# One GpSimd power instruction per small reciprocal square root, in a kernel of two float32 transformer blocks

## The chip, the cores and the metric

The kernel runs on one core of one Trainium2 chip. The metric is the device time of one execution in microseconds (us): the median of three runs before the change is 1636.81 us (1635.35 to 1637.84). A core has a matrix engine (TensorE; PE in the rows, with its weight loads as PEld), three engines for elementwise work (VectorE, DVE; ScalarE, ACT; GpSimd, POOL) and a queue for transfers (SyncE, SP). Each engine takes its instructions in a fixed order and waits on semaphores for what others make.

## What is computed

Two blocks of two layers each, on 256 tokens of 1024 features, with batch 1, all in float32. The first block puts 16 meta tokens ahead, so it works on 272. Each of its layers is a mixer (a gated delta rule and a sparse attention side by side, gated) and a gated feed-forward network with a convolution; the second block has one layer of dilated attention beside a gated convolution, one of retention, and a feed-forward network behind each. What matters here is that every layer normalises by roots of means or sums of squares:

```python
def rms_norm(x, g):
    xf = x.astype(jnp.float32)
    y = xf * lax.rsqrt(jnp.mean(xf * xf, axis=-1, keepdims=True) + EPS)
    return (y * g.astype(jnp.float32)).astype(x.dtype)

def l2_norm(x):
    xf = x.astype(jnp.float32)
    return xf * lax.rsqrt(jnp.sum(xf * xf, axis=-1, keepdims=True) + EPS)
```

```python
for l in range(DEPTH):
    n = rms_norm(h, norm_mix[l])
    h = h + hybrid_mixer(n, ...).astype(h.dtype)
    n = rms_norm(h, norm_ffn[l])
    h = h + conv_gated_mlp(n, w_up[l], conv_ffn[l], w_down[l]).astype(h.dtype)
```

## The kernel before

The residual stream lies in SBUF in eight tiles of 128 features by 272 (later 258 or 256) tokens. Every large product is a loop over tiles of 128 features of the weight: `raw` loads a piece of 1 MB from HBM into one of two buffers, `parts` splits it into a high part `whi` (ScalarE, L256) and a low part `wlo` (VectorE, L257), four buffers of each, and `mm3` makes three matmuls of each pair of tiles (L276, L277, L278), so that the sum is nearly exact in float32. These matmuls, 256 to 272 columns wide, are most of the program.

The norm is pulled apart (`Norm`). The products start at once on the stream times the gain (`xh`, `xl`), and the factor of each token comes beside them: ScalarE squares, VectorE adds (L162), TensorE sums over the features by a product with ones (L168), VectorE turns the sum into the mean `nrm_u` (L170), `rsqrt` makes the factor `nrm_y`, and TensorE casts it to all partitions (`rowcast`, L352), from where ScalarE copies it as `rB`. What leaves a product is multiplied by `rB`.

`rsqrt` is called 32 times, each for a tile of 128 partitions (16 for the meta tokens) by 1 to 16 elements: for the 8 norms (`nrm`), in each of the two `mixer1` for the index keys (`ri`), the delta rule's keys (`rk`), the attention's keys (`rka`) and queries (`qsc`) and three times for the outputs of the delta rule (`ors`), in `even_mixer` for keys and queries (`erk`, `erq`), and twice for each of the four heads of `retention_mixer` (`brv`). Each call takes the bit pattern of its operand as a first guess (L247) and makes three Newton steps of three instructions each (L249, L250, L251), all on VectorE, each needing the one before.

The small work runs in chains that `tick` steps between the products. The order of each engine's queue isn't the source's: the tile framework's scheduler sets it when the program is built, from priorities and its own estimates of when each instruction can start, so another way of making a factor moves work around it on every engine.

Of the kernel before, what the change touches and what calls it, by code (L numbers as in the profile page):

```python
# [11 lines left out]
F32 = mybir.dt.float32  # L12
# [108 lines left out]
def bc(ap, n):  # L121
    """[p, a] -> [p, a, n], the last axis with stride 0."""
    return ap.unsqueeze(2).to_broadcast([ap.shape[0], ap.shape[1], n])


def mid(ap, n):
    """[p, a] -> [p, n, a], the middle axis with stride 0."""
    return ap.unsqueeze(1).to_broadcast([ap.shape[0], n, ap.shape[1]])


class Norm:
    """RMS norm of the residual stream: parts X of h*g at once; the mean u of the squares with eps, the factor r of
    each row, and rB, the factors on every partition, come from a chain that runs beside the first products."""
# [56 lines left out]
class K:  # L190
    def __init__(self, ctx, tc, ins, out):
# [6 lines left out]
        self.chains, self.later, self.held = [], [], None  # L198

# [20 lines left out]
    def evict(self):  # L220
        """Emits what takes the last product out of PSUM: a tile late, for the priority of the products."""
# [19 lines left out]
    def rsqrt(self, u, n, tag, bufs=None, rows=P):  # L241
        """1/sqrt of the small tile u[:, :n], from the bit pattern and three Newton steps."""
        V = self.nc.vector
        yi = self.small(n, tag + "_y", I32, bufs)
        a, b = self.small(n, "nwt_a")[:rows], self.small(n, "nwt_b")[:rows]
        y, u = yi.bitcast(F32), u[:rows]
        V.tensor_scalar(yi[:rows], u.bitcast(I32), -0.5, 1597463007.0, OP.mult, OP.add)  # L247
        for _ in range(3):
            V.scalar_tensor_tensor(a, y[:rows], -0.5, y[:rows], OP.mult, OP.mult)  # L249
            V.tensor_tensor(b, a, u, OP.mult)  # L250
            V.scalar_tensor_tensor(y[:rows], b, 1.5, y[:rows], OP.add, OP.mult)  # L251
        return y

    def split(self, hi, lo, src):
        """hi + lo == src, both float32r; src in SBUF or PSUM."""
# [3 lines left out]
    def raw(self, src, nk, nc_):  # L259
        """src [128, nk * nc_] of a laid out weight -> SBUF."""  # L260
# [4 lines left out]
    def parts(self, v):  # L265
        """A [128, k, c] piece of a weight -> its float32r parts."""
# [13 lines left out]
    def dense(self, w, X, ev, ncols=256, raw=None, kstep=8):  # L280
        """A unit [128, k * ncols] of a weight times X of up to 8 k tiles, outputs feature-major, one at a time."""
# [19 lines left out]
    def pieces(self, w, nkt):  # L301
        """The parts of a unit of 256 columns, four k tiles at a time."""
# [6 lines left out]
    def dense_pair(self, w, X, ev, tag, ahead=()):  # L309
        """A unit of 256 columns times X of many k tiles, two outputs at a time; ahead: pieces that are there already."""  # L310
# [12 lines left out]
    def dense_ts(self, w, X, ev, tag):  # L323
        """X (two token tiles) times a unit of 512 columns, outputs token-major."""
# [24 lines left out]
    def rowcast(self, ps, col, seg):  # L349
        """ps[:, token] = the column's value of the token, on every partition."""  # L350
# [5 lines left out]
    def ffn(self, hv, N, lead, w_up, conv, w_down, both, done=None):  # L356
        """lead: columns of X ahead of the tokens that are kept (they feed the gate's convolution alone)."""
# [58 lines left out]
def in_turn(*gens):  # L416
    """A chain whose steps are a step of each of the generators."""
# [10 lines left out]
def by_turns(*gens):  # L428
    """A chain that steps one of the generators at a time."""
# [10 lines left out]
def mixer1(k_, l, h, N, final, first=None):  # L440
# [33 lines left out]
    def stats(src, rows, at, key):  # L474
        """Sums of squares over the features, token-major, in columns of stat."""
# [13 lines left out]
    # small projections: index key (64), index weights (8), decay (4), beta (4)  # L489
# [3 lines left out]
    def small_chain():  # L493
# [9 lines left out]
        # index keys, on both halves of the partitions  # L503
# [20 lines left out]
        # decay and beta  # L524
# [1064 lines left out]
```

## Time and profile before

| | us |
|---|---|
| runs, median of 3 | 1636.81 |
| the profiled execution, span from first to last instruction | 1633.0 |
| TensorE busy in it | 1616.9 (99%) |
| VectorE busy | 1228.8 (75%) |
| ScalarE busy | 881.7 (54%) |
| GpSimd busy | 17.9 (1%) |
| mean granted clock of TensorE | 0.993 of full |

The span is the profiled execution's own; the run's time holds what lies around it as well. Busy time of an engine says only that it had an instruction in work. Which engine sets the end is read from the chain of waits and from what TensorE waits for. A clock column of 1.00 stands for 2.4 GHz, of 0.50 for 1.2 GHz; a matmul then takes twice as long.

### The profile page before, as it was taken

The page shows a single profiled execution, that of the slowest core. Times are in us where ns is not written, and L with a number is a line of the kernel's source. Part 1 is how long each engine was busy: PE and PEld are TensorE (multiplying, and loading weights), DVE is VectorE, ACT ScalarE, POOL GpSimd, SP SyncE. Part 2 cuts the span into 40 slices and gives each one's busy share as a digit, 9 for nine tenths or more (in the row PEclk, how much of TensorE's full clock was granted, in tenths as well). Part 3 has the DMA queues.
Part 4 walks back from the last instruction along what each step waited for, and adds up shares of the span by engine and source line. Part 5 has one row for each costly group of instructions (what it writes and reads, how often), then busy time and mean ns, then how long its engine had stood idle before and what let it go on. Part 6 is the DMA issues. An engine that isn't in the chain of part 4 may idle for free.

```text
span 1633.0 us, 31727 instructions
## 1 busy us (share of the span) xinstructions
PE 1616.9 (99%) x12702; PEld 1551.1 (95%) x12702; DVE 1228.8 (75%) x2653; ACT 881.7 (54%) x1534; POOL 17.9 (1%) x174
## 2 busy tenths in 40 slices
PE   7999999999999999999999999999999999999999
PEld 7989899999999989999999998999999888999999
DVE  6788578888557887588886549899956767689963
ACT  5565455555445664555554456566644444556642
POOL 0000000000000000000000000000000000000000
PEclk9999999999999999999999999999999999999999
DMA  5432235445553322245555543455555454545553
GB/s 207 155 113 74 100 107 178 164 173 180 163 185 130 130 104 78 78 155 181 181 181 187 200 173 128 165 185 194 175 182 186 161 175 155 174 173 194 184 183 127
DMA packets 38452, 258.00 MB, mean 158 GB/s; under 512 B 4384, under 2 KB 6816, under 8 KB 9120
## 3 DMA queue, kind: packets, MB, share of 16 engines
q1 hardware_dynamic: 37440, 253.79, 44.7%
q8 instruction: 100, 1.64, 0.4%
q10 hardware_dynamic: 864, 2.18, 0.3%
q14 instruction: 48, 0.39, 0.1%
HBM read 254.90 MB, written 1.05 MB: 157 GB/s over the span
## 4 chain that ended last, share of the span: by engine, by line
PE 96%; DVE 3%; ACT 1%; issue 0%; DMA 0%; SPq 0%; ACTq 0%; DVEq 0%
PE psd L276 20%; PE psd L277 20%; PE psd L278 20%; PE pss L276 3%; PE pss L278 3%; PE pss L277 3%; PE psn L276 3%; PE psn L278 3%; PE psn L277 3%; PE psn L752 1%; PE stat L481 1%; PE psd L338 1%; PE psd L339 1%; PE psd L340 1%; PE psn L339 1%; PE psn L338 1%
## 5 line engine op out<-in xcount | busy, mean ns | idle before, releaser
L256 ACT ACTIVATE whi<-raw 128x1024 fp32r<-128x1024 f32 (+1 forms) x487 | 508.3, 1044 | 569.6 <-PE psd L277 329.5
L257 DVE TENSOR_TENSOR wlo<-raw,whi 128x1024 fp32r<-128x1024 f32 (+1 forms) x487 | 585.6, 1203 | 223.2 <-ACT whi L256 218.3
L276 PE MATMUL psd<-xh,whi 128*128 128x256 f32 (+2 forms) x2384 | 695.6, 292 | 6.0 <-ACT whi L256 6.0
L278 PE MATMUL psd<-xh,wlo 128*128 128x256 f32 (+2 forms) x2384 | 684.2, 287 | 0.7 <-DVE wlo L257 0.7
L277 PE MATMUL psd<-xl,whi 128*128 128x256 f32 (+2 forms) x2384 | 682.8, 287 | 0.0
L276 PEld LDWEIGHTS psd<-xh,whi 128*128 128x128 f32 x2384 | 453.6, 190 | 13.9 <-ACT whi L256 6.0
L277 PEld LDWEIGHTS psd<-xl,whi 128*128 128x128 f32 x2384 | 455.1, 191 | 3.3 <-issue 1.7
L278 PEld LDWEIGHTS psd<-xh,wlo 128*128 128x128 f32 x2384 | 453.3, 190 | 1.8 <-DVE wlo L257 1.2
L278 PE MATMUL pss<-ah,wlo 128*128 128x256 f32 (+1 forms) x352 | 99.9, 284 | 0.0
L278 PE MATMUL psn<-ah,wlo 128*128 128x256 f32 (+1 forms) x352 | 99.9, 284 | 0.0
L276 PE MATMUL pss<-ah,whi 128*128 128x256 f32 (+1 forms) x352 | 99.9, 284 | 0.0
L276 PE MATMUL psn<-ah,whi 128*128 128x256 f32 (+1 forms) x352 | 99.9, 284 | 0.0
L277 PE MATMUL psn<-al,whi 128*128 128x256 f32 (+1 forms) x352 | 99.7, 283 | 0.0
L277 PE MATMUL pss<-al,whi 128*128 128x256 f32 (+1 forms) x352 | 99.7, 283 | 0.0
L276 PEld LDWEIGHTS pss<-ah,whi 128*128 128x128 f32 x352 | 66.5, 189 | 0.0
L276 PEld LDWEIGHTS psn<-ah,whi 128*128 128x128 f32 x352 | 66.5, 189 | 0.0
L277 PEld LDWEIGHTS pss<-al,whi 128*128 128x128 f32 x352 | 66.5, 189 | 0.0
L277 PEld LDWEIGHTS psn<-al,whi 128*128 128x128 f32 x352 | 66.5, 189 | 0.0
L278 PEld LDWEIGHTS pss<-ah,wlo 128*128 128x128 f32 x352 | 66.2, 188 | 0.0
L278 PEld LDWEIGHTS psn<-ah,wlo 128*128 128x128 f32 x352 | 66.2, 188 | 0.0
L374 ACT ACTIVATE gy<-gu,prm 128x256 f32<-128x256 f32 (+1 forms) x88 | 43.5, 498 | 3.9 <-DVE gu L371 3.7
L376 DVE SCALAR_TENSOR_TENSOR gy<-gu,prm,gy 128x256 f32<-128x256 f32 (+1 forms) x88 | 42.8, 487 | 2.1
(401 smaller groups left out, 2450.2 us busy)
## 6 DMA issues: line engine op xcount, KB each, us to landing
raw<-in_w_up_dram SPq DMA_DIRECT2D x44, 1024.0 KB, 4.8
raw<-in_ffn_w_up_dram SPq DMA_DIRECT2D x44, 1024.0 KB, 4.8
raw<-in_w_in_dram SPq DMA_DIRECT2D x26, 1024.0 KB, 4.8
raw<-in_w_gate_dram SPq DMA_DIRECT2D x16, 1024.0 KB, 4.8
raw<-in_w_down_dram SPq DMA_DIRECT2D x16, 1024.0 KB, 4.9
raw<-in_ffn_w_down_dram SPq DMA_DIRECT2D x16, 1024.0 KB, 4.9
raw<-in_even_w_in_dram SPq DMA_DIRECT2D x10, 1024.0 KB, 4.8
raw<-in_w_out_dram SPq DMA_DIRECT2D x8, 1024.0 KB, 4.7
```

Of the source, the lines that this page charges most:

```text
L256: self.nc.scalar.activation(hi, src, AF.Copy)
L257: self.nc.vector.tensor_tensor(lo, src, hi.bitcast(F32), OP.subtract)
L276: mm(ps, w[0], x[0], start=first, stop=False)
L277: mm(ps, w[0], x[1], start=False, stop=False)
L278: mm(ps, w[1], x[0], start=False, stop=last)
L338: mm(ps[m], h, hi[:, k, :], start=(kk == 0), stop=False)
L339: mm(ps[m], h, lo[:, k, :], start=False, stop=False)
L340: mm(ps[m], l, hi[:, k, :], start=False, stop=(kk == nkt - 1))
L374: A.activation(y, u[:, o:o + T], AF.Copy, scale=conv(0, c))
L376: V.scalar_tensor_tensor(y, u[:, o + 2:o + 2 + T], conv(2, c), y, OP.mult, OP.add)
L481: mm(stat[:n, at(s):at(s) + 1], sq[:rows, o:o + n], c["ones"][:rows, 0:1], start=True, stop=True)
L752: mm(cols(p3, w, a, 4)[:, hh], R[:n, hh, :n], cols(Z, w, a, 4)[:, hh], start=True, stop=True)
```

## The change

`rsqrt` no longer runs on VectorE. One GpSimd instruction (`tensor_tensor` with the operation `pow`) raises the tile to -0.5; the exponent is a column `mhalf` of -0.5, set once on GpSimd and read with stride 0. The rest of the diff takes comments and docstrings out, which shifts line numbers: a line of the kernel after from 252 on is 4 less than before (L256 is L252, L352 is L348).

```diff
@@ class K, __init__ @@
         self.chains, self.later, self.held = [], [], None
+        self.mhalf = self.cp.tile([P, 1], F32, name="mhalf")
+        self.nc.gpsimd.memset(self.mhalf, -0.5)
...
     def rsqrt(self, u, n, tag, bufs=None, rows=P):
         V = self.nc.vector
-        yi = self.small(n, tag + "_y", I32, bufs)
-        a, b = self.small(n, "nwt_a")[:rows], self.small(n, "nwt_b")[:rows]
-        y, u = yi.bitcast(F32), u[:rows]
-        V.tensor_scalar(yi[:rows], u.bitcast(I32), -0.5, 1597463007.0, OP.mult, OP.add)
-        for _ in range(3):
-            V.scalar_tensor_tensor(a, y[:rows], -0.5, y[:rows], OP.mult, OP.mult)
-            V.tensor_tensor(b, a, u, OP.mult)
-            V.scalar_tensor_tensor(y[:rows], b, 1.5, y[:rows], OP.add, OP.mult)
+        y = self.small(n, tag + "_y", F32, bufs)
+        self.nc.gpsimd.tensor_tensor(y[:rows], u[:rows], self.mhalf[:rows, 0:1].to_broadcast([rows, n]), OP.pow)
         return y
```

Every engine has the same instructions as before but for these: VectorE loses 320, GpSimd gains 32 `pow`, the memset of `mhalf` and one instruction that loads code (ISA), ahead of the first `pow`. Their order differs. Three places follow, in the built programs' order.

TensorE at the norm that begins layer 1 of the first block, before the change. `sacc` holds the summed squares, `psd` is a product's accumulator, `nrm_y` the factor. First the sums of the norm:

```order
L168 MATMUL pss_6049<-g0_77,sacc_6014 16x1
L168 MATMUL pss_6049<-g0_77,sacc_6014 128x1 x2
L278 MATMUL psd_6076<-xh3_5962,wlo_6073 128x272
L276 MATMUL psd_6076<-xh4_5966,whi_6072 128x272
L277 MATMUL psd_6076<-xl4_5967,whi_6072 128x272
```

The row cast comes 33 wide matmuls after the sums, and the last of them before it are these:

```order
L278 MATMUL psd_6111<-xh5_5970,wlo_6108 128x272
L276 MATMUL psd_6111<-xh6_5974,whi_6107 128x272
L277 MATMUL psd_6111<-xl6_5975,whi_6107 128x272
L352 MATMUL pss_6090<-g0_77,nrm_y_6056 128x16
L352 MATMUL pss_6090<-g0_77,nrm_y_6056 128x128 x2
```

The same place on TensorE after the change (L272 to L274 are the wide matmuls, L348 is the row cast):

```order
L168 MATMUL pss_5952<-g0_79,sacc_5917 16x1
L168 MATMUL pss_5952<-g0_79,sacc_5917 128x1 x2
L274 MATMUL psd_5968<-xh3_5865,wlo_5965 128x272
L272 MATMUL psd_5968<-xh4_5869,whi_5964 128x272
L273 MATMUL psd_5968<-xl4_5870,whi_5964 128x272
L274 MATMUL psd_5968<-xh4_5869,wlo_5965 128x272
L348 MATMUL pss_5982<-g0_79,nrm_y_5959 128x16
L348 MATMUL pss_5982<-g0_79,nrm_y_5959 128x128 x2
L272 MATMUL psd_5968<-xh5_5873,whi_5964 128x272
```

Four wide matmuls are left between the sums and the row cast. Counted at the eight norms in their order, 23, 25, 33, 25, 24, 26, 60 and 26 matmuls stood between before, and 0, 12, 4, 11, 4, 11, 5 and 4 stand there now.

VectorE in the retention mixer, at the first head's first group norm. `buv` is the variance with its epsilon, `brv_y` the factor, `bnb` the negative mean times the factor. Before:

```order
L1365 TENSOR_TENSOR buv_16167<-bmv_16165,repu_16108 128x1
L247 TENSOR_SCALAR brv_y_16169<-buv_16167 128x1
L249 SCALAR_TENSOR_TENSOR nwt_a_16170<-brv_y_16169 128x1
L250 TENSOR_TENSOR nwt_b_16171<-nwt_a_16170,buv_16167 128x1
L251 SCALAR_TENSOR_TENSOR brv_y_16169<-nwt_b_16171,brv_y_16169 128x1
...
L1368 SCALAR_TENSOR_TENSOR bnb_16182<-bmv_16165,brv_y_16169 128x1
L257 TENSOR_TENSOR wlo_16340<-raw_16337,whi_16339 128x1024
```

And after:

```order
L1361 TENSOR_TENSOR buv_15916<-bmv_15914,repu_15857 128x1
L1364 SCALAR_TENSOR_TENSOR bnb_15920<-bmv_15914,brv_y_15918 128x1
L253 TENSOR_TENSOR wlo_16067<-raw_16064,whi_16066 128x1024
L1357 BN_STATS bst_15945<-pss_15942 128x6
L1359 BN_AGGR bmv_15947<-bst_15945 128x2
```

The ten instructions are gone from between `buv` and `bnb`, and `bnb` needs the factor that GpSimd makes; the split of a weight stands behind it.

GpSimd at the program's start, after the change (before, the first memset of `xp` stood first here, and there was no row of L247):

```order
L200 MEMSET mhalf_67 128x1
L572 MEMSET xp_300 128x3
L632 MEMSET sel0_1402 128x16
L632 MEMSET sel1_1652 128x16
L247 ISA
L247 TENSOR_TENSOR nrm_y_208<-nrm_u_206,mhalf_67 128x3
L247 TENSOR_TENSOR ri_y_286<-ui_284,mhalf_67 128x3
L572 MEMSET xp_373 128x3
```

The code load stands ahead of the first `pow`, and memsets for the convolutions stand behind the second.

## Rows read from the trace of the kernel before

**Rows 1.** The page: busy us, share of the span, count by engine; chain that ended last.

```profile
PE 1616.9 (99%) x12702; PEld 1551.1 (95%) x12702; DVE 1228.8 (75%) x2653; ACT 881.7 (54%) x1534; POOL 17.9 (1%) x174
...
PE 96%; DVE 3%; ACT 1%; issue 0%; DMA 0%; SPq 0%; ACTq 0%; DVEq 0%
```

**Rows 2.** Waits of PE and PEld: who waited for what, total us, times, longest us.

```profile
PE psd L276 <- ACT whi L256: 6.0, 1, 6.0
PE psd L278 <- DVE wlo L257: 0.7, 1, 0.7
...
PEld pss L352 <- DVE nrm_y L251: 1.4, 5, 0.3
PEld psx L1385 <- DVE on L1376: 0.7, 1, 0.7
```

**Rows 3.** Windows: length, busy us by engine, granted clock, DMA share, GB/s.

```profile
14.00:21.20 7.20, 6.49 (x30) 6.14 (x30) 4.91 (x28) 1.41 (x4) 0.00 (x0) 0.53 0.71 269
41.50:45.10 3.60, 3.60 (x19) 3.60 (x18) 3.60 (x6) 1.94 (x3) 0.00 (x0) 0.53 0.30 73
516.00:523.00 7.00, 6.61 (x44) 5.95 (x43) 5.71 (x14) 3.02 (x6) 0.10 (x1) 0.51 0.48 153
604.80:608.30 3.50, 3.50 (x18) 3.50 (x18) 2.12 (x9) 1.78 (x9) 0.00 (x0) 0.51 0.75 274
```

**Rows 4.** Timeline of PE ahead of two of these: start us, us, instruction, count.

```profile
40.18 0.39 PE L560 MATMUL psn<-g_g,g 128*128 128x8 f32 x2
...
514.54 0.38 PE L559 MATMUL psn<-g_g,g 16*128 16x4 f32 x2
```

**Rows 5.** Whole span, one line of the kernel each (L247, then L251): DVE busy.

```profile
0.00:1633.00 1633.00, 5.16 (x32) 0.99 0.46 158
...
0.00:1633.00 1633.00, 15.09 (x96) 0.99 0.46 158
```

**Rows 6.** Waits of DVE, the longest.

```profile
DVE wlo L257 <- ACT whi L256: 218.3, 209, 3.5
```

**Rows 7.** Timeline of DVE at the first group norm of retention.

```profile
1272.99 0.15 DVE L247 TENSOR_SCALAR brv_y<-buv 128x1 int32<-128x1 int32 x1
...
1274.93 0.16 DVE L1368 SCALAR_TENSOR_TENSOR bnb<-bmv,brv_y 128x1 f32<-128x1 f32 x1
```

**Rows 8.** Timeline of DVE and PE at the norm of layer 1.

```profile
483.47 0.37 PE L278 MATMUL psd<-xh,wlo 128*128 128x272 f32 x1
483.65 0.16 DVE L170 TENSOR_SCALAR nrm_u<-pss 128x3 f32<-128x3 f32 x1 [0.88 <-PE pss L168]
483.99 1.22 DVE L257 TENSOR_TENSOR wlo<-raw,whi 128x1024 fp32r<-128x1024 f32 x1
484.06 0.29 PE L276 MATMUL psd<-xh,whi 128*128 128x272 f32 x1
487.74 0.16 DVE L251 SCALAR_TENSOR_TENSOR nrm_y<-nwt_b,nrm_y 128x3 f32<-128x3 f32 x1
487.95 0.28 PE L352 MATMUL pss<-g,nrm_y 16*128 16x16 f32 x1
```

**Rows 9.** Groups by form: busy us, mean ns of one, idle before.

```profile
L370 POOL MEMSET gu<- 128x2 f32 x88 | 8.5, 99 | 898.4 <-DVE gy L376 323.9 <-DVE h L1417 271.3 <-DVE sacc L162 183.5
L775 POOL MEMSET Y<- 128x512 f32 x4 | 2.1, 525 | 131.1 <-PE psn L752 131.1
L143 ACT ACT_TABLE_LOAD x1 | 1.3, 1283 | 3.5 <-DMA h<-in_xT_dram 3.5
```

**Rows 10.** Timeline at the start.

```profile
0.77 0.16 POOL L636 MEMSET sel<- 128x16 f32 x2
14.97 0.57 PE L276 MATMUL psd<-xh,whi 128*128 128x272 f32 x1
15.15 0.16 DVE L170 TENSOR_SCALAR nrm_u<-pss 128x3 f32<-128x3 f32 x1 [1.05 <-PE pss L168]
16.76 0.29 PEld L278 LDWEIGHTS psd<-xh,wlo 128*128 128x128 f32 x1 [1.01 <-DVE wlo L257]
```

## Prediction

> **What bounds the kernel now.** I read the page first: TensorE is busy 1616.9 of 1633.0 us, VectorE 75%, GpSimd 1%, and the chain that ended last runs 96% through TensorE [rows 1]. So a change on VectorE or GpSimd moves the time only where TensorE waits for it, or where it alters the clock that TensorE is granted. Next the waits of TensorE, product side and weight-load side [rows 2]: the largest is the 6.0 us at the start, which nothing here touches. Those that end with VectorE are 0.7 us for `wlo`, 0.7 us for `on`, and 1.4 us, in 5 pieces, of row casts (L352) waiting for the last Newton step (L251). That 1.4 us is all that the chains which the change replaces cost directly; with `on` and the sub-microsecond waits beside it, there are about 2 us to win from waits. Last the windows of the granted clock [rows 3]: four stretches stand at about half (1.2 of 2.4 GHz), 7.2, 3.6, 7.0 and 3.5 us long. The work in them takes twice its time, so they hold some 10 us. Shortly before the second and the third, TensorE ran the small matmuls with 4 and 8 columns (L559, L560) [rows 4].
>
> **What goes.** There are 32 calls of `rsqrt`: 8 norms, 7 in each of the two `mixer1` (14), 2 in `even_mixer`, 8 in `retention_mixer`. Each loses one L247 and three each of L249, L250 and L251, which take the same time: 5.2 + 3 x 15.1 = 50.4 us of VectorE [rows 5]. On the end's path lies only the 1.4 us above. VectorE has cover to spare: it waits 218.3 us for `whi` [rows 6], which says that it is ahead of its supply.
>
> As a delay the chain matters more than as busy time. In retention, where nothing stands between the steps, L247 starts at 1272.99 and the user of the result, L1368, at 1274.93: 1.94 us [rows 7]. At the norm of layer 1 other work is woven in: the mean `u` is written at 483.81 and the last Newton step at 487.90, and the row cast starts at 487.95 [rows 8]. One hand-over between engines thus takes 0.05 us.
>
> **What comes.** One `pow` on GpSimd for each of the 32, over 1 to 16 elements a partition, one memset, and a code load ahead of the first. No row shows a `pow`; call its length p. From below: a GpSimd memset of 2 elements takes 99 ns, one of 512 takes 525 ns, so the element count is no term here and an instruction cannot be shorter than about 0.10 us [rows 9]. [...] I take 1.0 us, the middle, since it has more in common with the chain than with a memset. I know no reason that rules out either end.
>
> **Where p stands on the path.** The order of TensorE's queue moves with the change, and this is the term that decides. Before, 23 to 60 matmuls stood between the sums of a norm (L168) and its row cast (L352). Now, in the order of the eight norms, it is 0, 12, 4, 11, 4, 11, 5, 4. At the norm of layer 1 the rows price it: the first matmul behind the sums starts at 483.47 and the fifth at 484.06, so TensorE would come to the row cast about there, while `u` is written at 483.81 [rows 8]. With two hand-overs the factor is there at 483.91 + p, so TensorE waits p - 0.15. Each further matmul takes off 0.12 to 0.13.
>
> - Three norms with 4 matmuls: 3 x (1.0 - 0.15) = 2.55 us.
> - One with 5: 0.73 us.
> - Two with 11 and one with 12: seven or eight more matmuls, about 0.9 to 1.0 us; the wait is p - 1.05 or less, nothing at p = 1.0.
> - The first, with none: TensorE is through the sums at 14.97, `u` is written at 15.31 [rows 10], so it waits p + 0.44 = 1.44 us. But 1.01 us was lost there already, waiting for `wlo` [rows 10], and VectorE can make that meanwhile; I count 0.43.
>
> Sum 3.71 us, less the 1.4 us that the row casts waited before: +2.3 us. Other row casts (`ri`, `rka`) and the transposes of `erk` keep at least some ten matmuls of cover, and cost nothing at p = 1.0.
>
> **VectorE's own waits.** At 19 places (`srk` 2, `nqs` 2, `od` 6, `eqs` 1, `bnb` 8) the user of the factor is on VectorE and now stands next to, or one or two instructions behind, what makes `u`. VectorE then stands for p + 0.1 with everything behind it in its queue, `wlo` among it, which TensorE wants. It stood 1.94 us in the chain before, so this is a gain up to p of about 1.8 and I cost it at nothing; the 218.3 us of waiting for `whi` are the cover [rows 6]. Without that cover each 0.1 us over 1.8 would cost 1.9 us over the 19 places.
>
> **GpSimd's queue.** It is in order, and a memset behind a `pow` now waits with it. These memsets (174 instructions, 17.9 us) run far ahead of their users and GpSimd is idle 99% [rows 1], so nothing. The code load stands after two `sel` memsets that start at 0.77 us and end at 0.93, and does not wait for VectorE; `u` comes at 15.31 [rows 10]. It has 14.4 us of cover. The nearest row of a load of functions is ScalarE's table, 1.28 us [rows 9]. Nothing for it, then.
>
> The Trainium skill, GPSIMD Engine Reference, section 2.1 (Instruction dispatch), gives about 6 us for the code load of a first call; by that estimate the load ends near 7 us, and the sum stays. No run here shows it yet.
>
> **The forecast.** 1633.0 + 2.3 = 1635.3 us of span. The median of the runs is 1636.81, 3.8 us over the span of the profiled execution, for what lies around it; so 1639.1 us. Between the ends: p = 0.10 removes the 1.4 us and adds no wait, 1635.4; p = 1.94 gives 1.37 + 3 x 1.79 + 1.67 + 2.5 (the three long ones) - 1.4 = +9.5, 1646.3. From p = 1.2 on the change is slower by over 0.2% (3.3 us, about what a measurement of this kernel can tell from none).
>
> **Rivals.**
>
> - *A dear power.* Software on GpSimd takes 1.3 us or more, and TensorE stands at the eight row casts: 1641 at 1.3, 1646 at 1.94; at 3 us, 8 places x 1.06 more and 19 places of 1.1 us on VectorE, of which a part shows, 1655. For it: nothing in the trace bounds a software loop. Against: the operands are tiny.
> - *Fewer half-clock stretches: faster.* In the new order the six matmuls of L559 and L560 stand in layer 0 behind 24 wide products, where two stood between them and the sums (L481) ahead; in layer 1 the small matmuls L704 and L713 of the first segment move away from them. If the second and third stretch vanish, half of 3.6 + 7.0 us comes back: 1639.1 - 5.3 = 1633.8, and with a power of 0.7 us (1637.6 by the sum) 1632.3. It decides if those windows show the full clock. Against: stretches of this kind also arise elsewhere.
> - *More half-clock stretches.* Sums, a wait of about 1 us and the row cast now stand together at four norms. TensorE fell to half around sums and a wait at the start [rows 3, 10]. Two new stretches of 3.5 us cost 3.5 us, of 7 us 7 us: 1642.6 to 1646.
> - *The power waits for VectorE.* `wlo` stands in VectorE's queue directly behind `u` (or one small instruction later) and takes 1.22 us [rows 8]. If GpSimd could not read its operands while it runs, a power issued late would wait up to 1.22 us more: 4 x 1.22 at the short norms, 4.9 us, so 1644.0. Against: `wlo` started at 483.99, 0.18 us after `u` was written, so the power would be first. A code load that takes over 14.4 us goes with this case; it costs its excess once.
>
> On that the Trainium skill, SBUF — State Buffer, section "SBUF: two separate sides", says that GpSimd and a VectorE instruction with two operands in SBUF take one shared pair of ports in turn, each for its whole length. `wlo` reads two SBUF tiles, so the rule speaks against this change: by it whichever starts first holds up the other. The trace of before has no GpSimd instruction that reads, so it cannot bear it out.
>
> **How the numbers follow.** Forecast (p from 0.7 to 1.3, the clock as it was) 0.42: 1637.6 to 1641.3, two thirds of it within 0.2%. Dear power 0.22. Faster by the clock 0.13, of which 0.02 stays within 0.2%. More half clock 0.12. Power or code load held up 0.11, of which 0.04 stays within. That gives faster 0.11, same 0.28 + 0.02 + 0.04 = 0.34, slower 0.55. The predicted time is that of the likeliest case, 1639. The forecast alone spans 1637 to 1642; the range that should hold 8 in 10 reaches down to the faster clock, 1632, and up into the dear power, 1652.
>
> **What would show it.** In the profile after: the length of L247 on GpSimd (step p); the waits of TensorE's weight load at the row cast on GpSimd's `nrm_y`, which should come to about 4 us at 4 to 5 norms; VectorE's waits on `brv_y`, `ors_y`, `srk`, about 1.1 us each with `wlo` still in time; VectorE busy near 1178 us; and the windows of half clock, four of them as before. It is wrong if the power is over 1.3 or under 0.5 us, if the waits at the row casts are not there, or if the sum of half-clock time differs by over 3 us.

## The result, and the profile after

The changed kernel takes 1649.1 us against 1636.7 before: ratio 1.0077, 95% interval 1.0063 to 1.0092. The kernel after once more (e9 below) gave 1648.8 against 1637.0, ratio 1.0076 (1.0063 to 1.0088). It is slower by 12 us; the forecast was 1639.0. The sign and the range (1632 to 1652) held, the size did not: +12.4 us for +2.3.

In the kernel after, the line numbers behind the removed lines are 4 lower: the products are L272 to L274, the split `whi` is L252, the subtraction `wlo` L253, the row cast L348. L247 is now the power.

The page, as in [rows 1]: busy us, share of the span of 1649.7 us, count, by engine.

```profile
PE 1623.1 (98%) x12702; PEld 1555.0 (94%) x12702; DVE 1196.3 (73%) x2333; ACT 882.5 (53%) x1534; POOL 54.8 (3%) x207
```

The span grew by 16.7 us (1633.0 to 1649.7, the slowest of the four executions; the others lie between 1645.4 and 1647.4, and the medians differ by 12.4 only). Of it TensorE is busy 6.2 longer with the same 12702 matmuls, and stands 10.5 longer (1633.0 - 1616.9 = 16.1 before, 26.6 after). VectorE lost 32.5 us of work and nothing came of it.

Where TensorE stands, as in [rows 2]: who waits for what, total us, times, longest.

```profile
PE pss L348 <- POOL nrm_y L247: 4.5, 4, 2.3
PE psn L729 <- DVE XT L717: 2.4, 2, 1.2
...
PE psn L888 <- DVE od L883: 1.9, 2, 1.0
PE pss L1202 <- POOL up L1243: 1.7, 1, 1.7
PE psn L852 <- DVE W L838: 1.0, 2, 0.5
PE pss L1161 <- DVE att L1163: 0.8, 1, 0.8
PE pss L348 <- POOL xp L572: 0.6, 1, 0.6
```

In the kernel before none of these places stood over 0.2 us on the product side. The names "up" and "xp" are memsets that happen to follow a power in GpSimd's queue; what TensorE waited for there is the power (`erk_y`, `nrm_y`), as the timelines below show. So 5.1 us are row casts of norms, and 7.8 us are waits inside the mixers that the prediction had put at nothing.

How long a power takes: groups of L247 by form, busy us, mean ns of one, idle before. `qsc` and `rk` have 12 elements a partition, `erk` and `erq` 16, `ors` 4, `brv` 1.

```profile
L247 POOL TENSOR_TENSOR rk_y<-uqk,mhalf 128x12 f32<-128x12 f32 x2 | 4.5, 2266 | 33.9 <-DVE uqk L897 33.9
...
L247 POOL TENSOR_TENSOR brv_y<-buv,mhalf 128x1 f32<-128x1 f32 x8 | 4.4, 544 | 144.2 <-DVE buv L1361 144.2
L247 POOL TENSOR_TENSOR ors_y<-ouo,mhalf 128x4 f32<-128x4 f32 x4 | 4.0, 1008 | 103.6 <-DVE ouo L881 103.6
...
L247 POOL TENSOR_TENSOR erk_y<-euk,mhalf 128x16 f32<-128x16 f32 x1 | 2.9, 2896 | 9.9 <-DVE euk L1195 9.9
L247 POOL TENSOR_TENSOR ors_y<-ouo,mhalf 16x4 f32<-16x4 f32 x2 | 2.0, 999 | 6.4 <-DVE ouo L881 6.4
```

From 544 ns at one element to 2896 at sixteen is (2896 - 544) / 15 = 157 ns for each further element; four elements give 544 + 3 x 157 = 1015 by that, against 1008, and twelve give 2271, against 2266 for `rk` (`qsc` takes 2390; as it starts, VectorE is in work on two tiles, see e1). Sixteen partitions take as long as 128 (999 and 1008).

One of the new waits in full, at `rk` of the first mixer: timeline of GpSimd, VectorE and TensorE (start us, length, instruction, idle before and releaser).

```profile
81.48 2.27 POOL L247 TENSOR_TENSOR rk_y<-uqk,mhalf 128x12 f32<-128x12 f32 x1 [17.04 <-DVE uqk L897]
83.78 0.17 DVE L901 TENSOR_TENSOR srk<-rk_y,uqk 128x12 f32<-128x12 f32 x1 [2.12 <-POOL rk_y L247]
84.02 1.22 DVE L253 TENSOR_TENSOR wlo<-raw,whi 128x1024 fp32r<-128x1024 f32 x1
85.16 0.64 DVE L712 SCALAR_TENSOR_TENSOR MT<-psn,bet,QT 16x16 f32<-16x16 f32 x4
86.52 0.21 DVE L717 TENSOR_TENSOR XT<-XT,g 16x64 f32<-16x64 f32 x1
86.78 0.25 PE L729 MATMUL psn<-g,XT 16*16 16x16 f32 x4 [1.21 <-DVE XT L717]
```

`srk` stands 2.12 us for the power, and VectorE's queue stands with it: a subtraction, `MT` and `XT` come late, though none of them uses `srk`. TensorE then waits 1.21 us for `XT`. The same happens in layer 1.

The half-clock stretches (windows: length, busy us by engine, granted clock, DMA share, GB/s), as in [rows 3], the first and three that stand behind a new wait:

```profile
13.70:23.80 10.10, 7.79 (x36) 7.64 (x37) 4.54 (x18) 2.59 (x7) 2.77 (x3) 0.50 0.36 126
88.80:92.20 3.40, 3.40 (x27) 3.12 (x24) 2.11 (x4) 1.99 (x5) 0.00 (x0) 0.51 0.38 96
...
559.80:563.20 3.40, 3.40 (x21) 3.12 (x22) 2.07 (x7) 1.73 (x5) 0.00 (x0) 0.50 0.23 46
...
1460.90:1464.30 3.40, 3.40 (x17) 3.40 (x18) 0.43 (x1) 0.89 (x2) 0.00 (x0) 0.50 0.00 0
```

There are seven in this execution (the others start at 143.4, 525.7 and 614.4), with 28.2 us of TensorE's work in 30.6 us; before, four with 19.4 in 20.5. What half clock costs is somewhat less than half: wide matmuls of 272 columns start every 0.125 us at the full clock (483.68 to 484.06 in [rows 8]) and every 0.227 us at half (89.76 to 91.58 here), 1.8 times and not twice as long. So a stretch of 3.4 us loses about 1.5 us, and the 8.8 us of work more in such stretches come to some 4 of the 6.2 us that TensorE was busy longer (estimates from these spacings).

### The profile page after: what moved, and what is told of

Read it like the earlier page. It is cut to its first block, busy times and chain, and to the rows that moved or that the text cites. A ratio compares the mean times of both kernels' runs of the same rounds, so it can differ in the third digit from the quotient of the medians.

```text
span 1649.7 us, 31460 instructions
## 1 busy us (share of the span) xinstructions
PE 1623.1 (98%) x12702; PEld 1555.0 (94%) x12702; DVE 1196.3 (73%) x2333; ACT 882.5 (53%) x1534; POOL 54.8 (3%) x207
## 4 chain that ended last, share of the span: by engine, by line
PE 88%; issue 5%; DVE 4%; POOL 1%; ACT 1%; DMA 1%; SPq 0%; POOLq 0%; DVEq 0%; ACTq 0%
PE psd L272 18%; PE psd L273 18%; PE psd L274 18%; PE pss L272 3%; PE pss L273 3%; PE pss L274 3%; PE psn L273 3%; PE psn L272 3%; PE psn L274 3%; PE psn L748 1%; DVE wlo L253 1%; PE psn L335 1%; PE psn L334 1%; PE psn L336 1%; PE stat L477 1%
## 5 line engine op out<-in xcount | busy, mean ns | idle before, releaser
L252 ACT ACTIVATE whi<-raw 128x1024 fp32r<-128x1024 f32 (+1 forms) x487 | 507.9, 1044 | 558.2 <-PE psd L273 329.7
L253 DVE TENSOR_TENSOR wlo<-raw,whi 128x1024 fp32r<-128x1024 f32 (+1 forms) x487 | 585.3, 1203 | 236.7 <-ACT whi L252 231.3
L272 PE MATMUL psd<-xh,whi 128*128 128x256 f32 (+2 forms) x2384 | 696.0, 292 | 6.2 <-ACT whi L252 6.2
L274 PE MATMUL psd<-xh,wlo 128*128 128x256 f32 (+2 forms) x2384 | 684.0, 287 | 0.3 <-DVE wlo L253 0.3
L272 PEld LDWEIGHTS psd<-xh,whi 128*128 128x128 f32 x2384 | 453.7, 191 | 14.9 <-ACT whi L252 6.2
L274 PEld LDWEIGHTS psd<-xh,wlo 128*128 128x128 f32 x2384 | 453.2, 190 | 1.8 <-issue 0.9
L272 PE MATMUL pss<-ah,whi 128*128 128x256 f32 (+1 forms) x352 | 99.8, 283 | 0.0
L274 PE MATMUL pss<-ah,wlo 128*128 128x256 f32 (+1 forms) x352 | 99.8, 283 | 0.0
L274 PE MATMUL psn<-ah,wlo 128*128 128x256 f32 (+1 forms) x352 | 99.7, 283 | 0.0
L272 PE MATMUL psn<-ah,whi 128*128 128x256 f32 (+1 forms) x352 | 99.7, 283 | 0.0
L272 PEld LDWEIGHTS pss<-ah,whi 128*128 128x128 f32 x352 | 66.5, 189 | 0.0
L272 PEld LDWEIGHTS psn<-ah,whi 128*128 128x128 f32 x352 | 66.4, 189 | 0.0
L274 PEld LDWEIGHTS psn<-ah,wlo 128*128 128x128 f32 x352 | 66.2, 188 | 0.0
L274 PEld LDWEIGHTS pss<-ah,wlo 128*128 128x128 f32 x352 | 66.2, 188 | 0.0
L367 DVE TENSOR_TENSOR gu<-psd,rB 128x256 f32<-128x256 f32 (+2 forms) x88 | 37.4, 425 | 15.0 <-PE psd L274 9.6
```

Of the source, the lines that this page charges most:

```text
L252: self.nc.scalar.activation(hi, src, AF.Copy)
L253: self.nc.vector.tensor_tensor(lo, src, hi.bitcast(F32), OP.subtract)
L272: mm(ps, w[0], x[0], start=first, stop=False)
L274: mm(ps, w[1], x[0], start=False, stop=last)
L367: V.tensor_tensor(u[:, 2:2 + n], ps, N.rB, OP.mult)
```

## The experiments

Four questions: does the length of the power cost the time, or the new order of the queues? Which powers? Do GpSimd and VectorE hold each other up? Does a first call cost something? In e1 to e9 the order of the instructions on TensorE, VectorE and ScalarE is exactly that of the kernel named (after, or before in e2), so that only the stated thing differs.

**e1: the order of the kernel after, with a short instruction.**

```
-            V.memset(ps[:, 0:1], 1e30)
+            V.memset(ps[:, 0:1], 1.0)
...
-        self.nc.gpsimd.memset(self.mhalf, -0.5)
+        self.nc.gpsimd.memset(self.mhalf, 0.05)
...
-        self.nc.gpsimd.tensor_tensor(y[:rows], u[:rows], self.mhalf[:rows, 0:1].to_broadcast([rows, n]), OP.pow)
+        self.nc.gpsimd.tensor_tensor(y[:rows], u[:rows], self.mhalf[:rows, 0:1].to_broadcast([rows, n]), OP.mult)
```

> The kernel after with a product by a constant, 0.05, where each power stood (and 1.0 for the 1e30 of padded rows, so that all numbers stay finite; the factors are therefore not the roots). TensorE, VectorE and ScalarE run their instructions in exactly the order of the kernel after; only the length of the 32 GpSimd instructions changes. Theory A (the length of the power, at places where somebody stands for it): TensorE's waits for GpSimd (about 5 us at row casts, 1.7 at the transposes of erk) and the waits of VectorE for rk, qsc, ors, erq shrink to a few tenths each, the half-clock stretches that follow such a wait (88.8, 559.8, 1460.9) go, and the time falls from 1649.1 to 1637 to 1641. Theory B (the new order of the queues itself, with the clock that it brings): the time stays at 1645 or above, with the same seven half-clock stretches. Theory C (GpSimd's reading and VectorE's reading hold each other up): the norms at 15.97 and 1459.08, where a subtraction was already running on VectorE, still take a microsecond more than the others.

Measured: 1636.3, ratio to before 0.9996 (0.9986 to 1.0005). The product takes 0.19 to 0.22 us for 1 to 16 elements where nothing holds it up. Of TensorE's waits for a factor that are over 0.2 us only those at two row casts are left, 2.5 us, the places of theory C:

```profile
PE pss L348 <- POOL nrm_y L247: 2.5, 2, 1.6
```

Theory A holds, B falls: the new order, with its row casts 0 to 12 matmuls behind the sums, costs nothing by itself. Theory C, about single places, holds too: timeline at the first norm and, behind it, the next product of the same size.

```profile
15.51 1.22 DVE L253 TENSOR_TENSOR wlo<-raw,whi 128x1024 fp32r<-128x1024 f32 x1
15.55 1.24 POOL L247 TENSOR_TENSOR nrm_y<-nrm_u,mhalf 128x3 f32<-128x3 f32 x1 [14.59 <-DVE nrm_u L170]
...
16.88 0.19 POOL L247 TENSOR_TENSOR ri_y<-ui,mhalf 128x3 f32<-128x3 f32 x1
```

A product that takes 0.19 us takes 1.24 where a subtraction started 0.04 us ahead of it, and ends just behind that one's end (16.73, then 16.79). At the last norm it takes 1.12.

**e2: the kernel before, with the powers beside it** (`mhalf` as in the kernel after).

```
             V.scalar_tensor_tensor(y[:rows], b, 1.5, y[:rows], OP.add, OP.mult)
+        beside = self.small(n, "beside")
+        self.nc.gpsimd.tensor_tensor(beside[:rows], u, self.mhalf[:rows, 0:1].to_broadcast([rows, n]), OP.pow)
```

> The kernel before, whole, with the power of the same argument computed on GpSimd beside each Newton chain, and its result used by nobody. The order on TensorE, VectorE and ScalarE is exactly that of the kernel before. Theory A: nobody stands for the power, so the time is that of before, 1636.7, within 1.5 us, although GpSimd does all the work of the change. Theory C (GpSimd's reads cost VectorE or TensorE something while they run): slower by 3 us or more, with longer VectorE instructions beside the powers. The lengths should again be about 0.39 us plus 0.157 us an element, and longer only where a large VectorE subtraction had started first.

Measured: 1637.2, ratio 1.0001 (0.9992 to 1.0011). The page:

```profile
PE 1616.9 (99%) x12702; PEld 1550.5 (95%) x12702; DVE 1228.3 (75%) x2653; ACT 881.7 (54%) x1534; POOL 53.2 (3%) x207
```

GpSimd does all 32 powers (53.2 us busy against 17.9 before), and TensorE's and VectorE's busy times are those of [rows 1] to half a microsecond. The work of the powers costs nothing here; standing for them does. The lengths were to be longer only behind a large subtraction, and that was wrong: 29 of the 32 are 0.39 us plus 0.157 us an element to within 0.05, but three, at 98.35, 146.66 and 503.59, take 1.01, 2.69 and 1.06 for 0.85, 2.27 and 0.85, each while VectorE was in smaller work on two or more tiles (`sc`, `XT`, `yv`).

**e3: each power twice.**

```
-        self.nc.gpsimd.tensor_tensor(y[:rows], u[:rows], self.mhalf[:rows, 0:1].to_broadcast([rows, n]), OP.pow)
+        first = self.small(n, "first")
+        for o in (first, y):
+            self.nc.gpsimd.tensor_tensor(o[:rows], u[:rows], self.mhalf[:rows, 0:1].to_broadcast([rows, n]), OP.pow)
```

> The kernel after with each power computed twice, one behind the other on GpSimd, the second being the one that is used. The order on the other engines is unchanged. Theory A: every place where somebody stands for the power stands longer by its length. The powers take 36.9 us in all; without retention's eight (4.4) and the two pairs that TensorE does not wait on directly that leaves 15 to 28 us more, 1664 to 1677, and what is left over is what the cover hides. Theory B: under 5 us more, at most 1654, since the length matters little.

Measured: 1691.4, ratio 1.0331 (1.0314 to 1.0347), more than any theory said. Page and waits of TensorE (line numbers two higher than in the kernel after):

```profile
PE 1635.8 (97%) x12702; PEld 1566.3 (93%) x12702; DVE 1196.3 (71%) x2333; ACT 882.3 (52%) x1534; POOL 92.9 (6%) x239
```

```profile
PE pss L350 <- POOL nrm_y L249: 11.8, 7, 3.1
PE psn L731 <- DVE XT L719: 6.9, 2, 3.4
```

One of its windows:

```profile
90.00:97.00 7.00, 7.00 (x51) 6.13 (x50) 4.41 (x13) 2.77 (x6) 0.00 (x0) 0.51 0.52 186
```

TensorE stands 53.0 us, 26.4 more than in the kernel after: that part lies inside the 15 to 28 of theory A. The rest is the clock. TensorE is busy 12.7 us longer than in the kernel after, in eleven half-clock stretches; the one shown and one at 571.2 follow the waits for `XT`. I had counted waits only. In three points, with the same order: 1636.3 at about 0.2 us each, 1648.8 with the power, 1691.4 with two. That the second length costs more than three times the first would fit cover that the first has used up; this was not measured by itself.

**e4: one more power at the very start.**

```
         self.nc.gpsimd.memset(self.mhalf, -0.5)
+        warm = self.cp.tile([P, 3], F32, name="warm")
+        self.nc.gpsimd.memset(warm, 2.0)
+        self.nc.gpsimd.tensor_tensor(warm, warm, self.mhalf[:, 0:1].to_broadcast([P, 3]), OP.pow)
```

> The kernel after with one more power, of a constant, at the very start of GpSimd's queue, used by nobody. The order elsewhere is unchanged. The first norm's power took 1.91 us where the others of three elements take 0.85. If that is the cost of a first call (code load), the extra power takes it, the first norm's takes 0.85 us, and the time falls by about 1 us, to 1648. If it is the subtraction that VectorE started 0.03 us earlier (theory C), the first norm's power takes 1.9 us again and the time is unchanged, 1649.1.

Measured: 1647.6, ratio 1.0064 (1.0050 to 1.0078), an interval that overlaps that of the kernel after. Timeline of GpSimd and of VectorE's subtraction (line numbers three higher behind the added lines):

```profile
1.02 0.86 POOL L203 TENSOR_TENSOR warm<-warm,mhalf 128x3 f32<-128x3 f32 x1
...
15.77 0.85 POOL L250 TENSOR_TENSOR nrm_y<-nrm_u,mhalf 128x3 f32<-128x3 f32 x1 [13.90 <-DVE nrm_u L170]
15.81 1.24 DVE L256 TENSOR_TENSOR wlo<-raw,whi 128x1024 fp32r<-128x1024 f32 x1
```

The first norm's power took 0.85 here, as the theory of a first call expected. But the extra power, now the first of the run, took 0.86 and paid nothing; and the subtraction started 0.04 us behind the norm's power this time, not ahead of it. So the norm's 0.85 fits both theories and tells them not apart. The first row does: no cost of a first call is in the length of a power, nor in a gap ahead of it, for the two instructions that load code (MODIFY_POOL_CONFIG) start at 0.9 us, and the power at 1.02. That the 1.91 us were the subtraction's doing is shown by e1, not by this run.

**e5 to e8: the power in one group of calls, the product in the others.** The edit of e5; e6 has `nrm` in the list of names, e7 `ri`, `rka`, `ors`, e8 `brv`. `cheap` is a column of 0.05 (in e6 0.0005), and in e5, e7 and e8 the 1e30 is 1.0 as in e1.

```
-        self.nc.gpsimd.tensor_tensor(y[:rows], u[:rows], self.mhalf[:rows, 0:1].to_broadcast([rows, n]), OP.pow)
+        op, by = (OP.pow, self.mhalf) if tag in ("rk", "qsc", "erk", "erq") else (OP.mult, self.cheap)
+        self.nc.gpsimd.tensor_tensor(y[:rows], u[:rows], by[:rows, 0:1].to_broadcast([rows, n]), op)
```

> The order of the kernel after; the power stays in the six calls with 12 or 16 elements (rk and qsc in both mixers, erk, erq), the other 26 are the cheap product (by 0.05, and 1.0 for the 1e30 of padded rows; factors that are not roots). Against the 1636.3 of the all-cheap kernel. From the waits of the kernel after: XT 2.4 (VectorE stood 2.1 us for rk), the transposes of erk 1.7, att 0.8 behind erq, and two half-clock stretches of 3.4 us behind those XT waits, 1.7 each: 8.3 us, so 1644.6 (theory A1, the long powers carry two thirds of the loss). Theory A2 (the loss is at the row casts of the norms, as the prediction had it): under 1638. Theory A3 (each power costs alike, 12.8 / 32 = 0.4): 2.4 us, 1638.7.

> The order of the kernel after; the power stays in the eight norms alone, the other 24 are the cheap product (by 0.0005; factors that are not roots). From the kernel after: the waits at the row casts are 4.5 us against 2.5 with the product, and one more half-clock stretch follows the last (1461), 1.7: 3.7 us, so 1640.0 (A1). A2 (the row casts carry the loss): 1646 or more. A3: 3.2 us, 1639.5.

> The order of the kernel after; the power stays in the ten calls with 3 or 4 elements inside the mixers (ri, rka, ors), the other 22 are the cheap product (by 0.05, and 1.0 for 1e30; factors that are not roots). From the kernel after: od 1.9, W 1.0 and xp 0.6 of waiting, against 0.4 with the product: 3.1 us, so 1639.4 (A1). A2: no more than 1637. A3: 4.0 us, 1640.3.

> The order of the kernel after; the power stays in the eight calls of retention with one element, the other 24 are the cheap product (by 0.05, and 1.0 for 1e30; factors that are not roots). VectorE stands 5.7 us for them in the kernel after, 2.8 with the product, but no wait of TensorE follows but 0.5 for on: under 0.5 us, 1636.3 to 1636.8 (A1 and A2). A3: 3.2 us, 1639.5. The sum of the losses of these four kernels, if they add up, is the 12.8 us between the kernel after and the all-cheap one.

| power in | calls | time us | against 1636.3 | ratio to before | TensorE stands us |
|---|---|---|---|---|---|
| none (e1) | 0 | 1636.3 | | 0.9996 | 15.4 |
| e5: 12 and 16 elements | 6 | 1642.2 | +5.9 | 1.0027 (1.0018 to 1.0036) | 22.0 |
| e6: norms | 8 | 1638.4 | +2.1 | 1.0004 (0.9994 to 1.0014) | 18.5 |
| e7: ri, rka, ors | 10 | 1637.6 | +1.3 | 1.0002 (0.9993 to 1.0011) | 18.3 |
| e8: retention | 8 | 1636.8 | +0.5 | 0.9993 (0.9983 to 1.0003) | 15.8 |

(The last column is the span of the profiled execution less TensorE's busy time.) The medians stand in A1's order, and e8 is as it said; e5, e6 and e7 came out some two microseconds below it. Each ratio is good to about 0.001, that is 1.5 us, so by time only e5 is clear of e1; that the norms and `ri`, `rka`, `ors` cost something is seen in the standing (18.5 and 18.3 against 15.4), not in the time. A2 falls: the norms alone cost about a sixth of the loss, the six long powers about half. A3 falls at e5. The expectation of e7 also took the 0.6 us named `xp` for its own; it is the row cast of layer 1 and came with e6. The standing times add up to 6.6 + 3.1 + 2.9 + 0.4 = 13.0 us, against the 11.0 by which the kernel after (26.4 in its second profile) exceeds e1. The times add up to 9.8 of 12.5 us; where the other 2.7 went is not settled, but the stretches of half clock differ between executions of one kernel (five in the second profile of the kernel after, none at 1461, against seven), and each of 3.4 us is worth about 1.5 us, one of twice that length twice as much.

In e5 TensorE's waits for `XT`, `erk` and `att` stand exactly as in the kernel after (line numbers three higher):

```profile
PE psn L732 <- DVE XT L720: 2.4, 2, 1.2
...
PE pss L1205 <- POOL up L1246: 1.7, 1, 1.7
PE pss L1164 <- DVE att L1166: 0.8, 1, 0.8
```

**e9: the kernel after once more.**

> The kernel after itself, unchanged, so that it stands in one comparison with the next two. All theories: 1647 to 1651, the seven half-clock stretches not all in the same places in each execution.

Measured: 1648.8, ratio 1.0076 (1.0063 to 1.0088), a span of 1646.9 in its profile, with TensorE busy 1620.5 and standing 26.4. Its waits for the powers and in the mixers repeat those of the first profile to 0.1 us; its half-clock stretches are five, at 15.5, 87, 141.5, 558 and 613.

**e10: the users of the long powers on GpSimd.**

```
-        V.tensor_tensor(srk, rk, uk, OP.mult)
+        nc.gpsimd.tensor_tensor(srk, rk, uk, OP.mult)
...
-        V.tensor_scalar(nqs, qsc, -1.0, None, OP.mult)
+        nc.gpsimd.tensor_scalar(nqs, qsc, -1.0, None, OP.mult)
```

> The kernel after, with the two small products that use the long powers, srk (from rk) and nqs (from qsc), moved from VectorE to GpSimd, behind the power that they need; VectorE then no longer stands 2.1 us at each of four places with MT and the subtractions behind it. The powers are as long as before, and TensorE's order differs in a few places only. If VectorE's standing is what makes TensorE wait for XT: that wait (2.4 us in 2) goes, with the half-clock stretch behind each (1.7 us lost each), and the time is 3 to 6 us under the kernel after, 1643 to 1646. If TensorE waits for XT for another reason (the order): no change, 1649.

Measured: 1644.7, ratio 1.0050 (1.0037 to 1.0062), 4.2 us under e9 in the same comparison. Timeline at the same place:

```profile
81.39 2.26 POOL L247 TENSOR_TENSOR rk_y<-uqk,mhalf 128x12 f32<-128x12 f32 x1 [17.04 <-DVE uqk L897]
83.08 0.64 DVE L712 SCALAR_TENSOR_TENSOR MT<-psn,bet,QT 16x16 f32<-16x16 f32 x4
83.73 0.40 POOL L901 TENSOR_TENSOR srk<-rk_y,uqk 128x12 f32<-128x12 f32 x1
...
85.65 0.25 PE L729 MATMUL psn<-g,XT 16*16 16x16 f32 x4
```

The order moves in a few places with this edit. The power is as long as in the kernel after, `MT` runs during it and not 2 us behind it, and TensorE no longer waits. The stretches at 88 and 558 are gone with the wait. Stretches there stand in every profile with this wait (the kernel after twice, e3, e4, e5) and in none without it (before, e1, e2, e6, e7, e8, e10, e11).

**e11: the six long ones by Newton again** (`newton` is the `rsqrt` of before).

```
+        if not (n <= 4):
+            return self.newton(u, n, tag, bufs, rows)
         y = self.small(n, tag + "_y", F32, bufs)
```

> The power for the 26 calls with up to 4 elements, the ten VectorE instructions of before for the six with 12 or 16 (rk, qsc, erk, erq). The order of the queues is a new one, between the two kernels. From the kernels with the power in one group alone: 1636.3 + 2.1 for the norms + 1.3 for ri, rka, ors + 0.5 for retention = 1640 (theory A1). If the order had a price of its own after all, it is 1643 or more; a version faster than before, under 1634, is not expected, since TensorE had only about 2 us of waits to win.

Measured: 1640.3, ratio 1.0020 (1.0011 to 1.0029), as the sum of the groups said (to less than the noise of its terms); an order with a price of its own, 1643 or more, falls. TensorE stands 4.5 us for the row casts, 1.9 for `od` and 1.0 for `W`, each as in the kernel after, and no longer for `XT`, `erk` or `att`. It is 8.6 us better than the kernel after, and still slower than before. No experiment points to a version that beats the kernel before: e1, where the roots cost next to nothing, is its equal.

## Why the prediction was right or wrong

**The number.** The time lies in the range partly by luck. The range reached up to 1652 for a dear power, priced in the main by TensorE's waits at the eight row casts. What came is a dear power in six other calls, inside the mixers (e5, +5.9 us), which the forecast had put at nothing; the norms alone (e6) stay within noise of the kernel before. Without the six (e11) the time is 1640.3, near the 1639 of the forecast, but a part of that, too, are waits in the mixers (`od`, `W`) that it had at nothing.

**What bounds the kernel.** Right. VectorE's lost work is worth nothing: e1, with almost none of it on any engine, takes the time of before. One reading was off without harm to the sum: the 3.8 us between the span of the profiled execution and the median are not all "what lies around it". Every run is 1.7 to 1.9 us longer than its own span; the rest is that the profiled execution was one of the faster ones.

**The work removed.** The 50.4 us are a sum of lengths; VectorE's busy time fell by 32.5 only and stands at 1196, not "near 1178". Small neighbours overlap in the records: in the trace of before, VectorE's busy time without the 320 instructions is 1199.1 us, so only 29.7 of the 50.4 us were theirs alone. Here in the kernel after (timeline of VectorE and GpSimd at the norm of layer 1) `epu` takes 0.17 us, and the next VectorE instruction starts 0.07 us behind its start:

```profile
490.93 0.17 DVE L497 TENSOR_SCALAR epu<-nrm_u 128x3 f32<-128x3 f32 x1
490.97 0.85 POOL L247 TENSOR_TENSOR nrm_y<-nrm_u,mhalf 128x3 f32<-128x3 f32 x1 [5.14 <-DVE nrm_u L170]
491.00 1.24 DVE L253 TENSOR_TENSOR wlo<-raw,whi 128x1024 fp32r<-128x1024 f32 x1
```

**The length p.** This is the step that failed. "The element count is no term here" was read from memsets of 2 and 512 elements [rows 9], and a memset says nothing of what a power does with an element. No row of before shows a power, so none shows the 1.0 us that the sum goes by; the runs showed 0.54 to 2.90 us by size, and say nothing of how a power is made. The mean, 37.2 / 32 = 1.16 us, lies by the 1.0; but the six calls with 12 and 16 elements take 2.27 to 2.90. One length for all 32 was the error. The rival of the dear power (1.3 us or more) came true for these six, and the time lies between its 1646 and 1655, though not by the eight row casts from which those were in the main worked out.

**The row casts.** The rule of the prediction (p - 0.15 with four matmuls between, p - 0.27 with five, nothing with eleven or twelve) holds with the measured lengths. Layer 1, p = 0.85: 0.70 expected, 0.57 measured (the row of 0.6 above). The fifth norm, p = 0.70: 0.55 and 0.5; the seventh: 0.43 and 0.3; the second, fourth and sixth: no wait. The first and the last were held up by VectorE (below); with the 1.06 and 0.92 us of that added, the rule gives 2.35 and 1.47 for the measured 2.31 and 1.38. The gross 4.72 us of the prediction stand against 5.1. Of these 2.0 us are the holding up. And the 1.4 us that were taken off as saved [rows 2] were waits of the weight load alone; on the product side no row cast stood before. Even so e6 puts the norms' whole price at +2.1 us over e1, near the +2.3 of the forecast; with 1.5 us of noise on either time, and 2.0 us of holding up that the sum did not have, the agreement is partly luck. The waits at the norms were foreseen; the mixers were left out.

**The cover of erk.** "At least some ten matmuls of cover, and cost nothing at p = 1.0": 12 matmuls are there, and the power is 2.90 us, so TensorE stands 1.72 us.

```profile
963.72 2.90 POOL L247 TENSOR_TENSOR erk_y<-euk,mhalf 128x16 f32<-128x16 f32 x1 [9.94 <-DVE euk L1195]
964.58 1.23 DVE L253 TENSOR_TENSOR wlo<-raw,whi 128x1024 fp32r<-128x1024 f32 x1 [0.94 <-ACT whi L252]
966.67 0.38 PE L1202 MATMUL pss<-g,erk_y 128*8 128x128 f32 x2 [1.72 <-POOL up L1243]
```

**VectorE's own waits.** "A gain up to p of about 1.8 and I cost it at nothing." For retention that is right (e8: within 0.5 us). For the rest it failed twice. VectorE's waits for the power in the kernel after (who for what, total us, times, longest; "up" is again a memset behind the power):

```profile
DVE od L883 <- POOL ors_y L247: 5.8, 6, 1.2
DVE bnb L1364 <- POOL brv_y L247: 5.7, 8, 0.7
DVE nqs L998 <- POOL qsc_y L247: 4.3, 2, 2.2
DVE srk L901 <- POOL rk_y L247: 4.2, 2, 2.1
DVE eqs L1219 <- POOL up L1243: 3.0, 1, 3.0
```

Five of them, at `srk`, `nqs` and `eqs`, are of 2.1 to 3.0 us, beyond that bound. And the comparison with a chain of 1.94 us was false where other work is woven into the chain, as here before the change at `rk` of the first mixer (timeline of VectorE), where `ruk`, `iq`, `MT` and others run between the steps:

```profile
81.27 0.21 DVE L716 SCALAR_TENSOR_TENSOR MT<-psn,bet,QT 16x16 f32<-16x16 f32 x1
81.41 0.15 DVE L249 SCALAR_TENSOR_TENSOR nwt_a<-rk_y 128x12 f32<-128x12 f32 x1
```

There VectorE did not stand, and now it does, with all that is behind it in its queue. The 218 us of waiting for `whi` are a total; at this place `MT` and `XT` were late, not `wlo`. e10 shows it: without the standing the waits for `XT` go. Waits for `od` and `W` (2.9 us) are the same kind behind powers of 1.0 us, below the bound; e7 shows them with their group alone, at 1.3 us of time, which is within noise.

**GpSimd's queue and the code load.** Right: memsets behind a power made nobody wait, and a first call cost nothing in time. The Trainium skill, GPSIMD Engine Reference, section 2.1, gives about 6 us for the code load of a first call to newly loaded code; e4's first power, at 1.02 us, took 0.86, and the second, 14.8 us later, 0.85, and the two code loads start 0.1 us ahead of the first, so the trace shows none of it, neither in the length of a call nor ahead of one.

**The power waits for VectorE.** The prediction held against this rival that the power would be first. At two of the eight norms it was second:

```profile
1458.91 1.23 DVE L253 TENSOR_TENSOR wlo<-raw,whi 128x1024 fp32r<-128x1024 f32 x1
1459.08 1.62 POOL L247 TENSOR_TENSOR nrm_y<-nrm_u,mhalf 128x2 f32<-128x2 f32 x1 [4.57 <-DVE nrm_u L170]
...
1460.76 0.49 PE L348 MATMUL pss<-g,nrm_y 128*128 128x128 f32 x1 [1.38 <-POOL nrm_y L247]
```

The power of two elements takes 1.62 us here and 0.70 at the other three norms of that size; at the first norm 1.91 against 0.85. So 0.92 + 1.06 us of the row casts' 5.1 are this rival's. That is two fifths of the 4.9 us that it was priced at, and at the first norm a matter of 0.03 us in who starts first (e4's row is the other case). The Trainium skill, SBUF — State Buffer, section "SBUF: two separate sides", says that whichever of a GpSimd instruction and a VectorE instruction with two SBUF inputs starts first has the shared ports to itself until it ends. The trace bears out one half, that the later power waits for the subtraction. It contradicts the other, and the measurement decides: a subtraction that starts 0.03 us behind a power of 0.85 us, or in the middle of one of 2.90 us, takes 1.24 and 1.23 us, and the mean of all 469 of that size (1024 elements a partition) is 1.22.

**The clock.** The rival with fewer stretches fell: the one around 610 stayed, and the one around 520 stands in one of the two profiles of the kernel after. The one at 41.5 is gone and one at 143 is there that the profile of before has not; but e2, in the order of before, has the one and lacks the other too (windows of e2):

```profile
134.90:138.30 3.40, 3.40 (x18) 3.40 (x17) 0.82 (x4) 2.20 (x10) 1.00 (x1) 0.50 0.73 280
41.60:45.00 3.40, 3.40 (x29) 3.40 (x28) 3.16 (x6) 2.27 (x3) 0.00 (x0) 1.00 0.30 41
```

So neither needs the change to explain it. The rival with more stretches came true in part, by another cause than it named: two new ones, at 88.8 and 559.8, followed the waits in the mixers, not those of the norms. The one at 1461 did follow a norm, but in one only of six profiles with the same wait of 1.4 us there.

## What to carry to other kernels

Before an operation is moved to an engine whose price for it is unknown, look for its price per element and keep the calls of different size apart: a mean that fits can hide the six calls that cost. And where a short chain that other work was woven through becomes one long instruction on another engine, look at the user of its result: the queue in which it stands is stopped for the whole length, whoever needs the result. Work put beside the path cost nothing here, as e2 shows with the same powers; give the wait to a queue that nobody stands behind, as e10 does.

## What was not expected of the hardware

- A GpSimd power takes 0.54 us for one element a partition and 0.157 us more for each further one, 2.90 at 16, the same on 16 and on 128 partitions, where VectorE is not in work on two tiles as it starts; a product in its place takes 0.19 to 0.22 us at 1 to 16 elements.
- A GpSimd instruction that starts 0.03 to 0.17 us behind a VectorE subtraction of two SBUF tiles ends behind it (1.62 for 0.70, 1.24 for 0.19), while the subtraction that starts second is not lengthened: those that start within a power of the kernel after take 1.22 to 1.24 us, and the mean of all is 1.22.
- Half clock can follow a wait: one of 1.2 us or more ahead of small 16 x 16 matmuls (`XT`) was followed in each of ten cases (two places, five profiles) by a stretch of some 3.4 us or more at a granted clock of 0.5, that is at 1.2 GHz, in which TensorE loses about 1.5 us more (an estimate from the spacings above); e10 took away the wait, and the stretch went. Not every wait does it: none followed the 1.72 us at `erk`, in all five profiles with that wait, and the 1.4 us at the last norm had one behind it in one profile of six.
